# Order of a first tile's steps, longer warm-up, shift sums taken singly, and a fold split moved in a Fourier mixer layer

## The chip, the cores and the metric

The kernel runs on one core of one Trainium2 chip. The metric is device time in microseconds (us) of one execution, as the median of several; lower is better. The engines are called TensorE (PE in the profile, its weight loads PEld), VectorE (DVE), ScalarE (ACT), GpSimd (POOL) and SyncE (SP), which issues nearly all transfers.

## What is computed

One adaLN-modulated Fourier mixer layer on two sequences, 128 context tokens and 512 latent tokens of width 1024, each with a condition vector of its own:

```python
def modulation(cond, w_mod, b_mod):
    m = jax.nn.silu(cond) @ w_mod + b_mod
    shift, scale, gate = jnp.split(m[:, None, :], 3, axis=-1)
...
h = rms_norm(x, norm_w) * (1 + scale) + shift
u, z = jnp.split(h @ w_in, 2, axis=-1)          # w_in: 1024 x 2048
y = fourier_mix(u) * jax.nn.silu(z)             # real 2-D DFT over positions and 256 channels, 4 groups
return x + gate * (y @ w_out)                   # w_out: 1024 x 1024
```

All arrays are float32. Where full precision is wanted the kernel splits an operand into a high and a low part and makes three products (high x high, high x low, low x high).

## The kernel before, in words

The order of the work on every engine is written out by hand: each engine runs its instructions in the order in which the Python code issues them, and the framework only adds the semaphores. A helper `at(n, i, ...)` puts calls into a table, and `run(n, i)` issues them at that place of the loops over TensorE's products.

**First stage, z half of `w_in`, pieces 0 to 7** (lines 817 to 858). The width is cut into 8 tiles of 128. For each tile k there arrive `wm[k]` (512 KB of the scale weights), `xt[:, k]` (320 KB of transposed tokens) and piece k of `w_in` (256 KB, kept in `zs` for k < 5). From these come: `modulate(k)`, 16 small matmuls that give the scale (L285); `modulate_rows`, a ScalarE copy (L291); `modulate_columns`, 2 matmuls on TensorE (L295) and a VectorE step that gives `a8` (L296); `plain`, the high part of the scaled tokens `hh` (L329 on ScalarE; for tile 0 the 512 latent columns on VectorE, L325); `high_piece` and `low_piece`, the split of the weights into `wh` (L208, ScalarE, for tile 0 VectorE) and `wl` (L215, VectorE); `plain_low`, the low part `hl` (L336, VectorE). Then 12 matmuls of 512 columns (`product`, L358) and 3 for the context tokens (`product_ctx`, L368) per tile. The steps of tile u = k+1 are issued among the products of tile k. `ahead` says whether `modulate(u)` stands before or behind the first products of tile k; it is false for k = 0 and k = 6. `warm_up(n, cols)` issues matmuls on a tile of zeros (L269) whose result nobody reads.

**Shift sums.** The shift of each tile is a weighted sum taken on VectorE: `weigh_shift(k, j)` multiplies a 512 KB tile of weights with one of the two condition rows and accumulates (L302), and `finish_shift(k)` follows with three small steps (L310, L342, L343). `weigh_tile(k)` is two such sums and the finish. Tiles 0, 1 and 2 are weighed in the iterations k = 4, 5 and 6, behind `plain_low`; tiles 3 to 7 later. `load_shift(4)`, `(5)` and `(6)` reuse the memory of tiles 0, 1 and 2, so SP holds these transfers, and all behind them in its queue, until that tile is weighed.

**Second stage, pieces 8 to 15** (lines 890 to 926): 5 PSUM banks and 3 more hold 8 halves; `product_halves` fills them (L395). Beside it run the shift sums of tiles 3 to 7, the rms of the tokens, and the folds: `fold_pairs(q)` (8 VectorE steps) and `fold_split(q)`, which for each of 5 tables makes a ScalarE copy to f16 (L543) and a VectorE difference (L544), q being a quarter of the channels. `fold_piece(n)` is two VectorE steps on a piece of `w_in` (L201, L202), after which SP loads another piece. `take_halves(f, i)` copies a finished half from PSUM to `zs` (L442; VectorE for f = 1, ScalarE otherwise). `turn_shifts` makes 8 small matmuls (L421) into columns 256 to 263 of the bank that holds half (2, 1), and VectorE copies them out (L422). `sequence(k)` is 18 f16 matmuls (L569) into two PSUM tiles `pc` and `pl`, and `evacuate(k)` two ScalarE steps that empty them (L603). `sequence(0)` and `(1)` need fold quarter 0, `sequence(2)` quarter 1; `sequence(1)` takes over the PSUM tiles that `evacuate(0)` empties.

**The rest** (lines 929 to 1063): products for u (L609) with `sequence` between them, the channel transform, and the products with `w_out`, all of it TensorE work one behind the other.

Of the kernel before, what the change touches and what calls it, by code (L numbers as in the profile page):

```python
# [25 lines left out]
KT = D // P  # L26
# [78 lines left out]
def fourier_step(ctx: ExitStack, tc: tile.TileContext, a):  # L105
# [46 lines left out]
    def load_shift(k):  # L152
        if 0 <= k < KT:
            if k % 4 < 2:
                wr[k] = sp.tile([P, D], F32, name=f"wr{k}", tag="wr", bufs=2)
            else:
                wr[k] = folded[:, D * (k % 2) : D * (k % 2) + D]
            nc.sync.dma_start(wr[k], a["w_rows"][0, k])
# [9 lines left out]
    def load_piece(n):  # L168
        if n < 48 and n not in raw:
            c, k = place(n)  # L170
            src = a["w_in"][c, k] if c < 4 else a["w_out"][c - 4, k]
            if c == 0:
                if n < 5:
                    raw[n] = zs[:, 4:KT, :].rearrange("p e t -> p (e t)")[:, 512 * n : 512 * n + 512]
                else:
                    raw[n] = sp.tile([P, 512], F32, name=f"ws{n}", tag="wz", bufs=3)
                wz[n] = raw[n]
            else:
                raw[n] = wpool.tile([P, 512], F32, name=f"ws{n}", tag="ws")
            nc.sync.dma_start(raw[n], src)  # L180
# [24 lines left out]
    def high_piece(n, copy=nc.scalar.copy):  # L205
        if n < 48:
            hi = wpool.tile([P, 512], F32R, name=f"wh{n}", tag="wh")
            copy(hi, raw[n])  # L208
            wsplit[n] = (hi, None)

    def low_piece(n, engine=nc.vector):
        if n < 48:
            t, hi = raw.pop(n), wsplit[n][0]
            lo = wpool.tile([P, 512], F32R, name=f"wl{n}", tag="wl")
            engine.tensor_tensor(lo, t, hi, op=ALU.subtract)  # L215
            wsplit[n] = (hi, lo)
            if not (n < KT or 2 * KT <= n < 4 * KT):
                load_piece(n + 5)
# [48 lines left out]
    def warm_up(n, cols=512):  # L267
        for _ in range(n):
            nc.tensor.matmul(spare[:, 0:cols], idle[:, 0:P], idle[:, 0:cols], start=True, stop=True)  # L269
# [11 lines left out]
    def modulate(k):  # L281
        pm = pms[k % 2]
        for ko in range(KT):
            j = ko % 4
            nc.tensor.matmul(  # L285
                pm[32 * j : 32 * j + 32, 0:P], cs[:, ko, :], wm[k][:, ko, :], start=ko < 4, stop=ko >= 4
            )

    def modulate_rows(k):
        rows[k] = tmp.tile([P, P], F32, name="part")  # L290
        nc.scalar.copy(rows[k], pms[k % 2][:, 0:P])  # L291

    def modulate_columns(k):
        m = pms[k % 2][:, 256:258]
        nc.tensor.matmul(m, rows.pop(k), sel, start=True, stop=True)  # L295
        nc.vector.tensor_scalar(  # L296
            a8[:, k, :], m, b_scale[:, k : k + 1], nw8[:, k : k + 1], ALU.add, ALU.mult
        )

    def weigh(w, j, out):  # L300

        nc.vector.scalar_tensor_tensor(  # L302
            junk, w, 1.0, cb[:, D * j : D * j + D], ALU.mult, ALU.mult, accum_out=out
        )

    def weigh_shift(k, j):
        weigh(wr[k], j, sh[:, k, j : j + 1])

    def finish_shift(k):
        nc.vector.tensor_scalar(sh[:, k, :], sh[:, k, :], b_shift[:, k : k + 1], None, ALU.add)  # L310
        shift_columns(k, hs[k], T)
# [7 lines left out]
    def plain(k):  # L319
        hs[k] = tuple(  # L320
            xpool.tile([P, X_COLS], F32R, name=f"h{q}{k}", tag=f"a{q}") for q in "hl"
        )
        for j, cols in ((1, slice(0, SL)), (0, slice(SL, T))):
            if k == 0 and j:
                nc.vector.tensor_scalar(  # L325
                    hs[k][0][:, cols], xt[:, k, cols], a8[:, k, j : j + 1], None, ALU.mult
                )
            else:
                nc.scalar.activation(  # L329
                    hs[k][0][:, cols], xt[:, k, cols], AF.Identity, scale=a8[:, k, j : j + 1]  # L330
                )
# [8 lines left out]
    def shift_columns(k, parts, at):  # L340
        hi, lo = (x[:, at : at + 2] for x in parts)
        nc.vector.tensor_copy(hi, sh[:, k, :])  # L342
        nc.vector.tensor_tensor(lo, sh[:, k, :], hi, op=ALU.subtract)  # L343
# [9 lines left out]
    def product(n, f, act, passes=(0, 2, 1)):  # L353

        first, last = ends(n)
        for i in passes:
            w_, x_ = three(n, act)[i]
            nc.tensor.matmul(  # L358
                chunk(n // KT)[f], w_[:, P * f : P * f + P], x_[:, 0:SL],
                start=first and i == 0, stop=last and i == 1,  # L360
            )
# [427 lines left out]
    def go_ahead(k):  # L789
        if k < KT:  # L790
            load_scale(k)
            load_piece(k)
            load_tokens(k)
        if k == 3:
            load_cond()
        if k == KT:
            load_piece(KT)
            load_piece(KT + 1)
            load_shift(4)
            load_natural(0)  # L800
            nc.sync.dma_start(ident, a["ident"])
            load_natural(1)
        elif k > KT:
            load_shift(5)
            load_natural(2)
            for n in range(KT + 2, KT + 5):
                load_piece(n)
            load_natural(3)
        else:
            load_shift(k - 4)  # L810

    def weigh_tile(k):
        for j in range(2):
            weigh_shift(k, j)
        finish_shift(k)
# [3 lines left out]
    modulate(0)  # L819
    modulate_rows(0)  # L820
    warm_up(5, 128)
    high_piece(0, nc.vector.tensor_copy)
    modulate_columns(0)
    warm_up(6, 256)
    plain(0)
    low_piece(0)
    plain_low(0)
    for k in range(KT - 1):
        u = k + 1
        act = hs[k]  # L830
        ahead = 0 < k < KT - 2
        if ahead:
            modulate(u)
            modulate_rows(u)
        go_ahead(u + 2)
        for f in range(4):
            product(k, f, act, (0,))
        product_ctx(k, act, (0,))
        if not ahead:
            modulate(u)  # L840
            modulate_rows(u)
        high_piece(u)
        for f in range(2):
            product(k, f, act, (2,))
        modulate_columns(u)
        plain(u)
        low_piece(u)
        plain_low(u)
        if k == 2:
            silu_cond()  # L850
        if 3 < k:
            weigh_tile(k - 4)
        for f in range(2, 4):
            product(k, f, act, (2,))
        product_ctx(k, act, (2,))
        for f in range(4):
            product(k, f, act, (1,))
        product_ctx(k, act, (1,))
    k = KT - 1
    act = hs[k]  # L860
    high_piece(KT)
    low_piece(KT)
    load_shift(6)
    load_natural(4)
    product_ctx(k, act, (0,))
# [24 lines left out]
    for n, i, fn, *ms in (  # L890
        (8, 0, high_piece, 9), (8, 0, low_piece, 9), (8, 0, square, 0, 1), (8, 0, weigh_tile, 3), (8, 0, load_shift, 7),
        (8, 2, high_piece, 10), (8, 3, low_piece, 10), (8, 3, square, 2), (8, 3, load_tables),
        (9, 0, weigh_tile, 4), (9, 1, high_piece, 11), (9, 1, low_piece, 11), (9, 1, open_folds),
        (9, 1, weigh_tile, 5),
        (9, 2, square, 3), (9, 3, high_piece, 12, 13), (9, 3, low_piece, 12, 13), (9, 3, square, 4), (9, 3, rms),
        (10, 0, high_piece, 14), (10, 0, spread_rms), (10, 0, low_piece, 14), (10, 1, fold_first, 0),
        (11, 0, high_piece, 15), (11, 0, low_piece, 15), (11, 0, weigh_tile, 6, 7), (11, 0, fold_context, 0),
        (11, 2, fold_pairs, 0),
        (12, 1, fold_split, (0, "co", "so", "c", "ce", "se")),
        (12, 3, fold_first, 1), (12, 3, fold_context, 1),   # L900
        (14, 0, open_x, 0, 1, 2, 3), (14, 1, shift_products, 0, 1), (14, 1, order_rms), 
        (14, 1, take_halves, (0, 1), (0, 0), (3, 1)), (14, 1, fold_pairs, 1), (14, 1, fold_piece, 16), 
        (14, 2, take_halves, (3, 0)),  (14, 2, fold_piece, 17),
        (14, 2, fold_split, (1, "c", "co", "so", "se", "ce")),
        (14, 3, turn_shifts), (14, 3, load_gate, 0, 1), (14, 3, sequence, 0), (14, 3, take_halves, (1, 1), (2, 1), (1, 0)), (14, 3, evacuate, 0), (14, 3, fold_piece, 18),
    ):
        for m in ms or [()]:
            at(n, i, fn, *(m if type(m) is tuple else [m]))
# [33 lines left out]
    for n in range(16, 24):  # L942
        k = n - 16
# [187 lines left out]
```

## Time and profile before

| | us |
|---|---|
| median of 3 runs (lowest to highest) | 190.67 (190.64 to 191.15) |
| the profiled execution's own time | 192.47 |
| its span in the profile | 190.7 |

| engine | busy us | share of the span |
|---|---|---|
| PE | 182.9 | 96% |
| DVE | 145.3 | 76% |
| ACT | 87.8 | 46% |
| POOL | 16.8 | 9% |

The profile is of one execution. All times inside it count from the start of its span. "Busy" of PE is the union of its matmuls, whose starts are recorded and whose ends are modelled, so that one overlaps the next a little. "PEclk" is the share of TensorE's full clock, 2.4 GHz, that was granted in a stretch; the other level is 1.2 GHz. A number in brackets behind an instruction is the time for which its engine sat idle before it, and what ended that.

### The profile page before, as it was taken

The numbers are of one execution on the slowest core, as the hardware profiler recorded it, in microseconds if no ns is written. First come the engines' busy times: TensorE is split into PE (matmuls) and PEld (weight loads), VectorE is DVE, ScalarE is ACT, GpSimd is POOL, SyncE is SP. The second block draws the span as 40 slices with busy tenths as digits, with TensorE's granted clock in tenths as the row PEclk, the third lists the DMA queues.
The fourth block names the chain that finished last, engine by engine and source line by source line (L and its number), as shares of the span: only waits on it lengthen the run. The fifth ranks groups of instructions, "written<-read, shape, count | busy, mean of one in ns | idle before, by whom it ended". The sixth has DMA issues, their size and how long they took to land.

```text
span 190.7 us, 3251 instructions
## 1 busy us (share of the span) xinstructions
PE 182.9 (96%) x1162; PEld 147.5 (77%) x1162; DVE 145.3 (76%) x319; ACT 87.8 (46%) x195; POOL 16.8 (9%) x56
## 2 busy tenths in 40 slices
PE   7699999989999999799999999999999999999993
PEld 2467777768999979777767577677868889999993
DVE  0434435998999999969997696499869969999522
ACT  3133554347953039477626525868955127210000
POOL 3000000010033003700001103111110000000000
PEclk9879999999999999999999999999999999999999
DMA  5999999689983005752167613130142253712622
GB/s 187 354 410 405 404 401 403 232 295 366 348 283 141 8 3 155 236 229 64 52 199 216 235 58 107 55 110 5 58 108 57 83 181 137 241 76 109 238 106 100
DMA packets 15504, 35.55 MB, mean 186 GB/s; under 512 B 2432, under 2 KB 3200, under 8 KB 15360
## 3 DMA queue, kind: packets, MB, share of 16 engines
q1 hardware_dynamic: 15344, 35.30, 52.6%
q8 instruction: 9, 0.15, 0.4%
q10 hardware_dynamic: 144, 0.04, 0.1%
q14 instruction: 7, 0.06, 0.1%
HBM read 32.71 MB, written 2.62 MB: 185 GB/s over the span
## 4 chain that ended last, share of the span: by engine, by line
PE 65%; DVE 23%; ACT 5%; DMA 3%; issue 2%; SPq 1%; DVEq 0%
PE acc L358 21%; PE acc L609 14%; DVE junk L302 9%; PE h L395 8%; PE s L395 7%; PE acc L368 5%; PE pl L569 4%; DMA zs<-in_w_in 3%; DVE wl L215 2%; PE pm L285 2%; ACT hh L329 1%; DVE shz L310 1%; DVE hl L336 1%; PE acc L617 1%; PE pc L569 1%
## 5 line engine op out<-in xcount | busy, mean ns | idle before, releaser
L609 PE MATMUL acc<-x,folded 128*128 128x324 f32 (+1 forms) x128 | 37.0, 438 | 0.0
L609 PEld LDWEIGHTS acc<-x,folded 128*128 128x128 f32 x128 | 23.5, 190 | 9.6 <-issue 1.0
L215 DVE TENSOR_TENSOR wl<-ws,wh 128x512 fp32r<-128x512 f32 x27 | 17.9, 686 | 2.4 <-ACT wh L208 2.4
L302 DVE SCALAR_TENSOR_TENSOR junk<-wg,cb 128x1024 bf16<-128x1024 f32 x16 | 19.5, 1221 | 0.3
L208 ACT CAST wh<-ws 128x512 fp32r<-128x512 f32 x27 | 16.2, 616 | 7.6 <-PE h L395 7.5
L358 PE MATMUL acc<-yh,wh 128*128 128x512 f32 x32 | 13.1, 408 | 0.1
L358 PE MATMUL acc<-yl,wh 128*128 128x512 f32 x32 | 12.6, 394 | 0.0
L358 PE MATMUL acc<-yh,wl 128*128 128x512 f32 x32 | 12.6, 394 | 0.0
L329 ACT ACTIVATE hh<-xt,a 128x128 fp32r<-128x128 f32 (+1 forms) x15 | 7.5, 545 | 10.9 <-DVE a L296 10.9
L358 PE MATMUL acc<-hh,wh 128*128 128x512 f32 x32 | 10.3, 446 | 1.6 <-DVE hh L325 1.6
L296 DVE TENSOR_SCALAR a<-pm,b_scale,nw 128x2 f32<-128x2 f32 x8 | 2.2, 277 | 12.4 <-PE pm L295 12.4
L358 PE MATMUL acc<-hh,wl 128*128 128x512 f32 x32 | 11.1, 423 | 0.0
L395 PE MATMUL h<-hh,wl 128*128 128x256 f32 (+1 forms) x40 | 11.0, 292 | 0.0
L395 PE MATMUL h<-hl,wh 128*128 128x256 f32 (+1 forms) x40 | 11.0, 292 | 0.0
L395 PE MATMUL h<-hh,wh 128*128 128x256 f32 (+1 forms) x40 | 11.0, 292 | 0.0
L395 PE MATMUL h<-yh,wh 128*128 128x256 f32 (+1 forms) x40 | 11.0, 292 | 0.0
L395 PE MATMUL h<-yl,wh 128*128 128x256 f32 (+1 forms) x40 | 11.0, 292 | 0.0
L395 PE MATMUL h<-yh,wl 128*128 128x256 f32 (+1 forms) x40 | 11.0, 290 | 0.0
L302 DVE SCALAR_TENSOR_TENSOR junk<-folded,cb 128x1024 bf16<-128x1024 f32 x8 | 9.8, 1222 | 0.1
L302 DVE SCALAR_TENSOR_TENSOR junk<-wr,cb 128x1024 bf16<-128x1024 f32 x8 | 9.8, 1222 | 0.1
L358 PE MATMUL acc<-hl,wh 128*128 128x512 f32 x32 | 9.2, 393 | 0.0
L336 DVE SCALAR_TENSOR_TENSOR hl<-xt,a,hh 128x512 fp32r<-128x512 f32 (+1 forms) x16 | 8.1, 548 | 1.4 <-ACT hh L329 1.4
(212 smaller groups left out, 462.3 us busy)
## 6 DMA issues: line engine op xcount, KB each, us to landing
ws<-in_w_in SPq DMA_DIRECT2D x27, 256.0 KB, 4.5
wg<-in_w_rows SPq DMA_DIRECT2D x8, 512.0 KB, 3.4
ws<-in_w_out SPq DMA_DIRECT2D x16, 256.0 KB, 2.7
wm<-in_w_scale SPq DMA_DIRECT2D x7, 512.0 KB, 7.9
xt<-in_x_t SPq DMA_DIRECT2D x8, 320.0 KB, 7.7
xn<-in_x_nat SPq DMA_DIRECT2D x5, 512.0 KB, 6.1
out<-o SPq DMA_DIRECT2D x7, 320.0 KB, 2.2
wr<-in_w_rows SPq DMA_DIRECT2D x4, 512.0 KB, 6.9
```

The costliest lines, as they stand in the source:

```text
L208: copy(hi, raw[n])
L215: engine.tensor_tensor(lo, t, hi, op=ALU.subtract)
L285: nc.tensor.matmul(pm[32 * j : 32 * j + 32, 0:P], cs[:, ko, :], wm[k][:, ko, :], start=ko < 4, stop=ko >= 4)
L296: nc.vector.tensor_scalar(a8[:, k, :], m, b_scale[:, k : k + 1], nw8[:, k : k + 1], ALU.add, ALU.mult)
L302: nc.vector.scalar_tensor_tensor(junk, w, 1.0, cb[:, D * j : D * j + D], ALU.mult, ALU.mult, accum_out=out)
L329: nc.scalar.activation(hs[k][0][:, cols], xt[:, k, cols], AF.Identity, scale=a8[:, k, j : j + 1])
L336: nc.vector.scalar_tensor_tensor(hl[:, cols], xt[:, k, cols], a8[:, k, j : j + 1], hh[:, cols], ALU.mult, ALU.subtract)
L358: nc.tensor.matmul(chunk(n // KT)[f], w_[:, P * f : P * f + P], x_[:, 0:SL], start=first and i == 0, stop=last and i == 1,)
L368: nc.tensor.matmul(chunk(n // KT)[4], x_[:, SL:T], w_, start=first and i == 0, stop=last and i == 1)
L395: nc.tensor.matmul(half(c, f, j), w_[:, P * f : P * f + P], x_[:, tokens(c)[j]], start=first and i == 0, stop=last and i == 2,)
L569: nc.tensor.matmul(to, fold[source][x][rows, kk], t[rows, c : c + w], start=n == 0, stop=n == len(jobs) - 1)
L609: nc.tensor.matmul(chunk(n // KT)[f][:, 0 : cols.stop - cols.start], raw[n][:, P * f : P * f + P], xs[n % KT][:, cols], start=first, stop= ...
```

## The change

Five edits, all of order and place; the only added work is 8 matmuls on zeros.

1. Tile 0 on VectorE: `modulate_columns(0)` and `plain(0)` now stand ahead of `high_piece(0)`.
2. The last warm-up is 14 matmuls of 256 columns instead of 6.
3. The shift sums of tiles 0 to 2 become parts (tile i // 2, condition i % 2): part 0 in iteration 3, parts 1 and 2 in iteration 4, part 3 in 5, part 4 in 6, and part 5 behind `low_piece(8)` in the last tile's products.
4. `ahead` is true for k = 6 too: the scale of tile 7 stands before the products of tile 6.
5. In the second stage `take_halves(2, 1)` and `(1, 1)` go from behind `turn_shifts` and `sequence(0)` to the place (14, 2), before the last products of f = 1; `fold_split(1)` goes from (14, 2) to the end of (14, 3), behind `evacuate(0)` and `fold_piece(18)`; `take_halves(1, 0)` goes behind `evacuate(0)`.

```diff
+    def weigh_part(i):
+        weigh_shift(i // 2, i % 2)
+        if i % 2:
+            finish_shift(i // 2)
...
     warm_up(5, 128)
+    modulate_columns(0)
+    warm_up(14, 256)
+    plain(0)
     high_piece(0, nc.vector.tensor_copy)
-    modulate_columns(0)
-    warm_up(6, 256)
-    plain(0)
     low_piece(0)
     plain_low(0)
     for k in range(KT - 1):
         u = k + 1
         act = hs[k]
-        ahead = 0 < k < KT - 2
+        ahead = 0 < k
...
-        if 3 < k:
-            weigh_tile(k - 4)
+        for i in {3: (0,), 4: (1, 2), 5: (3,), 6: (4,)}.get(k, ()):
+            weigh_part(i)
...
     high_piece(KT)
     low_piece(KT)
+    weigh_part(5)
     load_shift(6)
...
-        (14, 2, take_halves, (3, 0)),  (14, 2, fold_piece, 17),
-        (14, 2, fold_split, (1, "c", "co", "so", "se", "ce")),
-        (14, 3, turn_shifts), (14, 3, load_gate, 0, 1), (14, 3, sequence, 0), (14, 3, take_halves, (1, 1), (2, 1), (1, 0)), (14, 3, evacuate, 0), (14, 3, fold_piece, 18),
+        (14, 2, take_halves, (3, 0), (2, 1), (1, 1)),  (14, 2, fold_piece, 17),
+        (14, 3, turn_shifts), (14, 3, load_gate, 0, 1), (14, 3, sequence, 0), (14, 3, evacuate, 0), (14, 3, take_halves, (1, 0)),
+        (14, 3, fold_piece, 18), (14, 3, fold_split, (1, "c", "co", "so", "se", "ce")),
```

## Rows read from the trace of the kernel before

**Rows 1.** Stretches of the span: start:end, length, busy us (instructions) per engine, clock, DMA.
```profile
4.80:8.20 3.40, 1.91 (x29) 1.21 (x21) 1.01 (x3) 0.67 (x2) 0.00 (x0) 1.00 0.97 335
8.20:11.60 3.40, 3.26 (x21) 2.09 (x21) 1.61 (x4) 0.00 (x1) 0.00 (x0) 0.50 1.04 408
...
46.00:79.00 33.00, 32.64 (x252) 31.02 (x251) 31.72 (x76) 17.34 (x42) 7.62 (x18) 1.00 0.54 175
...
80.00:187.60 107.60, 107.49 (x623) 86.55 (x620) 87.10 (x185) 50.15 (x112) 6.12 (x21) 1.00 0.37 125
```

**Rows 2.** Timeline of the first tile: start, duration, engine, line, instruction, [idle before].
```profile
1.19 3.17 PE L269 MATMUL spare<-idle 128*128 128x512 f16 x7 [1.19 <-DVE idle L232]
...
5.90 0.81 PE L269 MATMUL spare<-idle 128*128 128x256 f16 x6
...
7.15 0.43 DVE L208 CAST wh<-zs 128x512 fp32r<-128x512 f32 x1 [6.02 <-DMA zs<-in_w_in]
7.49 0.27 DVE L296 TENSOR_SCALAR a<-pm,b_scale,nw 128x2 f32<-128x2 f32 x1
...
7.80 0.49 DVE L325 TENSOR_SCALAR hh<-xt,a 128x512 fp32r<-128x512 f32 x1
...
8.34 2.08 PE L358 MATMUL acc<-hh,wh 128*128 128x512 f32 x4 [1.63 <-DVE hh L325]
...
11.74 0.73 PE L358 MATMUL acc<-hh,wl 128*128 128x512 f32 x2
```

**Rows 3.** Transfers of early tiles: issues on SP, and us from issue to landing.
```profile
1.65 0.42 SPq L162 DMA_DIRECT2D xt<-in_x_t  x1
2.59 0.43 SPq L150 DMA_DIRECT2D wm<-in_w_scale  x1
11.88 0.33 SPq L150 DMA_DIRECT2D wm<-in_w_scale  x1
...
xt<-in_x_t SPq DMA_DIRECT2D x1, 320.0 KB, 4.3
...
wm<-in_w_scale SPq DMA_DIRECT2D x1, 512.0 KB, 5.8
...
wm<-in_w_scale SPq DMA_DIRECT2D x7, 512.0 KB, 7.9
```

**Rows 4.** Timeline of TensorE in the next tile, same columns as rows 2.
```profile
14.44 0.64 PE L285 MATMUL pm<-wm,cs 128*32 128x128 f32 x16
...
16.28 0.63 PE L358 MATMUL acc<-hh,wl 128*128 128x512 f32 x2
```

**Rows 5.** Timeline from tile 5's scale to the start of tile 7.
```profile
30.52 0.28 DVE L296 TENSOR_SCALAR a<-pm,b_scale,nw 128x2 f32<-128x2 f32 x1 [2.38 <-PE pm L295]
...
38.86 1.22 DVE L302 SCALAR_TENSOR_TENSOR junk<-wr,cb 128x1024 bf16<-128x1024 f32 x1
...
40.68 0.27 DVE L296 TENSOR_SCALAR a<-pm,b_scale,nw 128x2 f32<-128x2 f32 x1
...
41.09 0.40 PE L368 MATMUL acc<-wh,hl 128*128 128x512 f32 x1
...
42.05 0.50 PE L368 MATMUL acc<-wh,hh 128*128 128x512 f32 x1 [0.57 <-ACT hh L329]
```

**Rows 6.** Timeline around `turn_shifts` and `sequence(1)`, by engine.
```profile
74.33 0.95 PE L421 MATMUL h<-small,shifts 128*128 128x2 f32 x8
...
78.29 0.34 PE L395 MATMUL s<-hh,wl 128*128 128x386 f32 x1
79.65 0.22 PE L569 MATMUL pl<-seq_h,co_h 128*128 128x128 f16 x1 [1.01 <-ACT x L603]
...
74.61 0.44 ACT L543 CAST c_h<-xn 128x256 f16<-128x256 f32 x1
...
78.95 0.37 ACT L442 COPY zs<-h 128x256 f32<-128x256 f32 x1 [2.48 <-DVE zs L422]
...
78.76 0.15 DVE L422 COPY zs<-h 128x8 f32<-128x8 f32 x1
```

## The prediction

> **What bounds the kernel now.** I read the table of stretches first. From 80 us to the end of the products TensorE is busy for 107.49 of 107.60 us, and from 46 to 79 us for 32.64 of 33.00 [rows 1]. So nothing late can be won without removing matmuls, which the change does not do; what can be won lies where TensorE stands still or runs slowly. Then I read the timelines of TensorE for gaps, and there are three. (1) The first tile: the warm-up ends at 6.7 us, the first product starts at 8.34 after 1.63 us of idleness [rows 2], and the granted clock, full from 4.8 to 8.2, is 0.50 (1.2 GHz) from 8.2 to 11.6 [rows 1]. In the 3.4 us before that fall TensorE was busy for 1.91 us. (2) At 42.05 us TensorE waits for tile 7's `hh` [rows 5]. (3) At 79.65 us `sequence(1)` waits for `evacuate(0)` [rows 6]. After 80 us a shift of everything in front passes unchanged to the end.
>
> **Edit 1, order on VectorE.** Today VectorE waits for piece 0, which has landed just before 7.15, then does the copy `wh` (0.43), the scale (0.27) and `hh` (0.49), and the product follows at 8.34 [rows 2]. The scale needs only TensorE's column step, which comes ahead of the 5.90 warm-up, so VectorE could do it at about 6.1. `hh` also needs the tokens, issued at 1.65 and landed 4.3 later, at 5.95 [rows 3]. In the new order scale and `hh` are through at about 6.9, under the wait for piece 0, and the copy runs from 7.15 to 7.58. The first product starts at about 7.62: **0.72 us earlier**.
>
> **Edit 2, warm-up.** 256 columns at 2.4 GHz take 0.107 us, so 14 matmuls from 5.90 end at about 7.4, inside the wait; their cost is nothing as long as they run at full clock, and the cover is the 0.2 us that is left to 7.62. The stretch from 4.8 to 8.2 will then be busy for about 2.9 of 3.4 us instead of 1.91. The clock had risen after a stretch filled like that (7 warm-ups over 3.17 us from 1.19 [rows 2]), so I take it that it does not fall at 8.2. What the fall costs is read at either level: from the first `hh,wh` to the third pass, five products of 512 columns and the 16 scale matmuls take 11.74 - 8.34 = 3.40 us [rows 2]; the same work of the next tile at full clock takes 16.28 - 14.44 = 1.84 [rows 4]. **1.56 us**, if no transfer is late: `wm[1]`, issued at 2.59, lands 5.8 later at 8.4 [rows 3], and is wanted at about 8.9. The next tiles' transfers are issued early: the one at 11.88, with 7.9 to land, is there by 19.8 [rows 3], and is wanted at some 21.0. Between 0 (the clock falls all the same) and 1.56 I take 1.56, since the stretch is closer to the filled one.
>
> **Edits 3 and 4, shift sums and `ahead`.** Today two sums and a finish stand between tile 6's work and tile 7's scale on VectorE. The second sum runs at 38.86 for 1.22 us, the scale comes at 40.68, and TensorE, whose last product started at 41.09, starts the next at 42.05 [rows 5]. A product of 512 columns is 0.21 us at full clock, so up to 0.96 - 0.21 = 0.75 us are lost (0.57 by the idle time alone, which takes modelled ends). VectorE's work is the same in sum. One sum moves into iteration 3, where VectorE idles for about 2.4 us per tile (2.38 before the scale at 30.52 [rows 5]), and one behind `low_piece(8)`. Iteration 4 has two sums and a finish and overruns a tile's 4.5 us by about half a microsecond, so tile 6's scale stays late by that much; but `modulate(7)` now stands before tile 6's products and fills 0.6 us in TensorE, so that nothing waits. Iteration 6 has one sum, begun after tile 7's `hl`. I take **0.75 us**, with 0.57 as the low end. On SP, `load_shift(4)`, `(5)` and `(6)` and what is queued behind them wait for tiles 0, 1 and 2. These are finished some 3 us earlier too, so no transfer of the second stage gets later against its use.
>
> **Edit 5, the fold split.** VectorE's 5 differences of `fold_split(1)` stand before `turn_shifts`' copy, which runs at 78.76. ScalarE's `take_halves(2, 1)` waits 2.48 us for that copy, `evacuate(0)` stands behind it on ScalarE, and TensorE, whose last product started at 78.29, starts `sequence(1)` at 79.65 [rows 6]. A product of 386 columns is 0.16 us, so 1.20 us are lost (1.01 by the idle time). With the split behind `evacuate(0)` this chain is gone: **1.20 us**. What is late next: quarter 1 of the fold is wanted only by `sequence(2)`, a round of TensorE's work later; I estimate that the differences end about 2 us ahead of it. But the edit adds a wait. `take_halves(2, 1)` reads the bank that `turn_shifts`' matmuls write, and now stands before them. ScalarE reaches that place at 74.61, when it begins the casts today, and the copy takes 0.37 [rows 6]; TensorE is ready at 74.33. It would start at about 75.03: **0.70 us back**, and all products stand queued behind. Between 0 (no order between the two) and 0.70 I take 0.70. For it speaks that today ScalarE's copy waits for VectorE's copy of other columns of that same bank, though both only read. The Trainium skill's page "PSUM — Partial Sum Buffer", section "PSUM bank collisions raise a hardware error", says that any two engines at one bank must be kept apart, reads against reads included. By that rule the 0.70 is due, and the trace's wait agrees with it; if only equal columns were kept apart, the sum would be 186.4.
>
> **Sum.** 0.72 + 1.56 + 0.75 + 1.20 - 0.70 = 3.53 us. The profiled execution took 192.47 us, its span of 190.7 and 1.8 around it; the median of the runs is 190.67. The profiled one would become 188.9, and the median 190.67 - 3.53 = **187.1 us**.
>
> **Rivals.**
> - *The clock gives nothing*, because it falls in spite of the longer warm-up, or did not fall in the unrecorded runs (they are 1.8 us shorter than the recorded one, which may be the recording alone). 187.1 + 1.56 = 188.7. For it: only one execution is seen. Against it: the stretch is filled as before the rise. Chance 0.16.
> - *The warm-up runs at 1.2 GHz*, because the clock rises later than at 4.8 in other executions. 14 times 0.213 from 5.90 ends at 8.9, 1.27 us behind 7.62: 188.4. The skill's page "TensorE: Matmul & The Clock Gate", part 1, says that the place of the rise differs from run to run; by that, some runs would be so. The three runs lie within 0.5 us. Chance 0.06.
> - *No wait at `turn_shifts`*: 187.1 - 0.7 = 186.4, if ScalarE's copy and TensorE's matmuls, in different columns, need no order. Chance 0.10.
> - *The head start is absorbed.* VectorE is busy for 31.72 of 33.00 us from 46 to 79 [rows 1]; if its chain kept its old times, TensorE would wait for it at `turn_shifts` and only edit 5 would be left: 190.67 + 0.70 - 1.20 = 190.2. Against it: VectorE starts that stretch behind TensorE's and ScalarE's last steps of the first stage, which come earlier by the same 3 us. Chance 0.06.
> - *Slower: the new wait at `turn_shifts` grows.* It lengthens one for one with any lateness of ScalarE behind VectorE's folds. The run is slower once the copy, which would end at 75.0 on the old clock, ends later than 74.33 + 1.20 + 0.57 = 76.1, that is when the fold chain is 1.1 us later than today in spite of the earlier start. 2 us later, it gives 190.67 + 2.0 + 0.70 - 1.20 = 192.2. It would take a shift sum, or a transfer held behind it on SP, that becomes late; the moved sums all come earlier, so I see none. Chance 0.04.
>
> **How the numbers follow.** The forecast has 0.58, with its own range of 186.8 to 187.7 from the ends 0.57 and 1.01. The range of 186.3 to 188.9 takes in the missing wait below and the two clock rivals above, and leaves out about 0.1. About 0.3% (0.6 us) is what a measurement of this kernel can tell from no change. The forecast, the two clock rivals and the missing wait are faster (0.90), the absorbed start is the same (0.06), the last is slower (0.04).
>
> **What the changed profile would show.** First product at 7.6 us, and a granted clock of 1.00 from 8.2 to 11.6 (a start at 7.6 with 0.50 behind it: the first rival; a start near 8.9: the second). Tile 7's first product near 39.0 with no idle time before it. The first stage ending some 3.0 us earlier. TensorE idle for about 0.7 us before L421, released by ScalarE's L442, at about 72.0; several microseconds there would be the absorbed start or the slower rival. `sequence(1)` at about 76.1 without a wait, and from there a constant shift to a span of about 187.2. I am wrong if a new wait stands between 46 and 80 us, or if the shift changes after 80.

## The result: 189.27 us, and the profile after

The changed kernel took 189.27 us in the median (188.94 to 189.36) beside 190.83 for the kernel before (190.64 to 191.15): ratio 0.9913, 95% interval 0.9894 to 0.9933, so 1.66 us less by the ratio (1.3 to 2.0). Forecast were 187.1 us and a range of 186.3 to 188.9. The direction was right, the size was under half of the 3.53 us that were forecast, and the time lies outside the range.

The odd thing is that the profile after is nearly the one that was forecast. Its span is 187.4 us (forecast about 187.2), its execution took 189.23. The span of before was 190.7, so the two profiles differ by 3.3 us, the two medians by 1.6. Each profiled execution is 1.8 us longer than its span; so the median of before, 190.83, belongs to a span of about 189.0, not of 190.7. Executions of the kernel before fall in two groups, one near 191 us and one from 192.35 up, and the profiled one was of the upper group.

The first tile after; the columns are start, duration, engine, line, instruction, [idle before]:

```profile
4.43 1.08 PE L285 MATMUL pm<-wm,cs 128*32 128x128 f32 x16
5.45 0.69 PE L269 MATMUL spare<-idle 128*128 128x128 f16 x5
...
6.17 1.69 PE L269 MATMUL spare<-idle 128*128 128x256 f16 x14
...
6.44 0.28 DVE L296 TENSOR_SCALAR a<-pm,b_scale,nw 128x2 f32<-128x2 f32 x1 [5.31 <-PE pm L295]
...
6.75 0.49 DVE L325 TENSOR_SCALAR hh<-xt,a 128x512 fp32r<-128x512 f32 x1
...
7.15 0.42 DVE L208 CAST wh<-zs 128x512 fp32r<-128x512 f32 x1
7.62 1.19 PE L358 MATMUL acc<-hh,wh 128*128 128x512 f32 x4
```

Beside [rows 2]: the first product starts at 7.62 as forecast, 0.47 us behind the start of the copy instead of 1.19, and four products take 1.19 us, not 2.08. The copy itself has no idle time before it any more: it follows `hh`, not the transfer, since the scale came at 6.44, 0.3 us later than I had worked out. In this execution the 16 scale matmuls took 1.08 us and ran at 1.2 GHz throughout; in the recorded one of before they took 0.76. The slack that I had left before the copy took this up, so that 7.62 came out all the same.

The stretches after (same columns as [rows 1]):

```profile
4.80:8.20 3.40, 3.40 (x40) 2.75 (x32) 1.69 (x4) 0.67 (x2) 0.00 (x0) 1.00 1.02 346
8.20:11.60 3.40, 3.40 (x30) 2.42 (x29) 1.98 (x6) 1.63 (x4) 0.00 (x0) 1.00 1.04 406
...
80.00:184.00 104.00, 103.89 (x595) 84.04 (x593) 85.32 (x180) 47.16 (x105) 6.11 (x21) 1.00 0.36 118
```

The granted clock stays at 1.00 where it was 0.50. From 80 us on TensorE is as full as before. Tile 7's start, then the place of `turn_shifts` and `sequence(1)`:

```profile
38.84 0.39 PE L368 MATMUL acc<-wh,hl 128*128 128x512 f32 x1
39.07 0.39 PE L368 MATMUL acc<-wh,hh 128*128 128x512 f32 x1
...
71.05 0.33 PE L395 MATMUL h<-hh,wl 128*128 128x386 f32 x1
71.97 1.05 PE L421 MATMUL h<-small,shifts 128*128 128x2 f32 x8 [0.59 <-ACT zs L442]
...
76.03 0.34 PE L395 MATMUL s<-hh,wl 128*128 128x386 f32 x1
76.21 0.23 PE L569 MATMUL pl<-seq_h,co_h 128*128 128x128 f16 x1
```

Against [rows 5] and [rows 6]: no wait for tile 7's `hh` (39.07, forecast 39.0); no wait before `sequence(1)` (76.21, forecast 76.1); and the new wait before L421, released by ScalarE's copy L442, at 71.97 (forecast 72.0). The lead over before is 79.65 - 76.21 = 3.44 us at `sequence(1)`, still 3.42 for matmuls at 160 us, and 3.28 for those at 167 us. So the sign "if the shift changes after 80" came in a small way: 0.14 us are lost there without a wait in the trace, and what took them is open.

### The profile page after: what moved, and what is told of

It reads as the page before. It is cut to its first block, busy times and chain, and to the rows that moved or that the text cites. A ratio compares the mean times of both kernels' runs of the same rounds, so it can differ in the third digit from the quotient of the medians.

```text
span 187.4 us, 3268 instructions
## 1 busy us (share of the span) xinstructions
PE 182.4 (97%) x1170; PEld 148.1 (79%) x1170; DVE 145.1 (77%) x319; ACT 87.6 (47%) x195; POOL 17.1 (9%) x56
## 4 chain that ended last, share of the span: by engine, by line
PE 76%; DVE 15%; ACT 6%; issue 1%; DVEq 0%
PE acc L358 25%; PE acc L609 14%; PE h L395 8%; PE s L395 8%; DVE junk L302 6%; PE acc L368 6%; PE pl L569 4%; PE spare L269 3%; PE pm L285 3%; DVE wl L215 2%; ACT zs L442 1%; PE pc L569 1%; PE acc L617 1%; ACT wh L208 1%; DVE shz L310 1%
## 5 line engine op out<-in xcount | busy, mean ns | idle before, releaser
L358 PE MATMUL acc<-hh,wh 128*128 128x512 f32 x32 | 9.4, 417 | 0.0
```

Of the source, the lines that this page charges most:

```text
L358: nc.tensor.matmul(chunk(n // KT)[f], w_[:, P * f : P * f + P], x_[:, 0:SL], start=first and i == 0, stop=last and i == 1,)
```

## The experiments

Two theories stood after the result. **A**: the fall of the clock belongs to the profiled execution, and most executions behind the median do not have it; its 1.56 us were taken off a time that did not contain them. **B**: the fall is in every execution, and the other terms were too large. Each kernel was run beside the kernel before on the same chip. The record has the mean granted clock of every execution: a fall to half for 3.4 of some 190 us makes it 0.991, and executions of before have either 0.991 and less or 0.997 and more. The ratios below are formed with executions of both groups. So the distance between the medians of the usual executions is given too, which are those with a mean clock of 0.997 or more and a time below 192 us; where the two differ, that distance is what an edit is worth.

**The kernel before, again.** No edit.

> The kernel before, unchanged, to see the span and the granted clock of many executions. Theory A (the fall of the clock at 8.2 us belongs to the one execution that the sum was made from): most executions have a span near 188.9 us, a mean clock of 0.999 or more and a time near 190.8; one with a mean clock near 0.991 would have a span near 190.7 and a time near 192.5. Theory B (the fall is in every execution, and other terms of the sum were too large): mean clock 0.991 in nearly all.

Twelve executions: five from 190.71 to 191.52, seven from 192.50 to 193.94, nothing between. The median of this set is 192.57, in the upper group, while only 4 of the 23 executions beside it are there (median 191.14); so the share changes from set to set. Over all sets of this study, the copy included, 100 timed executions of the kernel before lie so: 74 from 190.5 to 191.5 (median 191.0) and 26 from 192.35 up (median 192.7). Of the 96 whose clock is on record 23 have 0.982 to 0.991, all of them in the upper group; three of that group (192.35, 192.37 and 193.62) have 0.998 or more. The one recorded here is of the upper group, 193.94 with a span of 192.2. Its first copy and first product, and its stretches:

```profile
8.51 0.43 DVE L208 CAST wh<-zs 128x512 fp32r<-128x512 f32 x1 [7.38 <-DMA zs<-in_w_in]
...
9.70 1.20 PE L358 MATMUL acc<-hh,wh 128*128 128x512 f32 x4 [3.21 <-DVE hh L325]
```
```profile
4.10:10.90 6.80, 3.48 (x35) 2.28 (x34) 2.36 (x6) 0.89 (x4) 0.53 (x3) 1.00 1.01 366
10.90:14.30 3.40, 3.40 (x24) 2.50 (x23) 0.99 (x4) 1.18 (x3) 0.00 (x0) 0.51 1.05 413
```

The clock falls here too, but at about 10.9 us; piece 0 had landed some 1.4 us later (8.51 against 7.15), so that TensorE had been idle for 3.2 us before the first product. Theory A holds in its main point: the fall is not in every execution. It was not seen to be rare, though; a quarter have it, and in this set more than half.

**Longer warm-up alone.**

```diff
-    warm_up(6, 256)
+    warm_up(14, 256)
```

> The kernel before with 14 instead of 6 warm-up matmuls of 256 columns, nothing else. Theory A: the median stays within 0.3 us of before's (190.8), since there is no fall to prevent in most executions. Theory B: 1.5 us less, about 189.3. Third possibility: the warm-up runs at the low clock in part and delays the first product: up to 0.6 us more.

191.15 beside 191.14, ratio 1.0 (0.9985 to 1.0016); the usual executions beside it have 191.10. Theory B is out. But the eleven executions lie between 190.84 and 191.42, with none in the upper group; if a quarter of them were to have the fall, that would be luck about once in twenty such sets. So the edit probably does what it was costed for, in the executions that have the fall, and the median is not one of them. Its recorded execution is also what a profile of before without the fall looks like: its span is 189.5.

**No last warm-up.** The kernel before without the last 6 matmuls on zeros, to bring the fall about.

```diff
-    warm_up(6, 256)
```

> The kernel before without the last 6 warm-up matmuls, so that TensorE idles for about 2.4 us before the first product. If the fall of the clock follows from that idle time, nearly every execution has it: times near 192.5, a granted clock of 0.5 over some 3.4 us of the first two tiles, and 1.5 us more than the kernel before has in its usual executions (191.1). If the fall comes and goes for other reasons, the median stays at 191.1 with a few executions near 192.5, as before.

192.54 beside 191.03, ratio 1.009 (1.0061 to 1.0118), and 1.6 us above the usual executions (190.93); all eleven executions are at 192.28 or above. In the recorded one TensorE idles for 1.80 us before the first product, not for 2.4. Its stretches:

```profile
5.70:9.10 3.40, 1.60 (x11) 1.30 (x10) 2.13 (x5) 0.59 (x2) 0.00 (x0) 1.00 1.03 381
9.10:12.50 3.40, 3.40 (x23) 2.18 (x23) 0.78 (x4) 0.78 (x2) 0.00 (x0) 0.50 1.03 411
```

By the mean clock (0.991 or less) the fall is in 8 of 11 executions without the last warm-up, in 23 of 96 with 6 matmuls and in 0 of 11 with 14. Its price, between the groups' medians of before, is 1.7 us; the 1.56 of the sum was about right. The other three executions here (193.37, 193.61 and 193.82) have a mean clock of 0.999, like the three of before: they are long without a fall in the record, and why is open. A first rise that comes late would not show in that number, since the clock column reads 1.00 from the start, also over the first seven warm-ups of before (columns as in [rows 1]):

```profile
1.20:4.40 3.20, 3.15 (x7) 0.85 (x7) 0.00 (x0) 1.75 (x4) 0.69 (x4) 1.00 0.72 236
```

These seven matmuls of 512 columns take 3.17 us [rows 2], 0.45 each, about twice the 0.23 from one such product to the next at full clock (38.84 and 39.07 in the first section); so they ran at 1.2 GHz.

**The changed kernel with 6 warm-ups.**

```diff
-    warm_up(14, 256)
+    warm_up(6, 256)
```

> The changed kernel with the old 6 warm-up matmuls. Theory A: the median is that of the changed kernel, 189.2, within 0.3 us; single executions may still have a fall, since the first product comes at 7.6 and the idle time before it is shorter. Theory B: 1.5 us more, 190.8.

189.15 beside 191.14 (ratio 0.9894, 0.9867 to 0.992), 1.95 us below the usual executions, and none of its five above 189.43. No gain of the long warm-up is seen in the changed kernel: the new order of the first tile has already cut the idle time before the first product, to 0.63 us in the recorded execution:

```profile
7.15 1.19 PE L358 MATMUL acc<-hh,wh 128*128 128x512 f32 x4 [0.63 <-DVE wh L208]
```

**The first tile's order alone.**

```diff
-    high_piece(0, nc.vector.tensor_copy)
     modulate_columns(0)
     warm_up(6, 256)
     plain(0)
+    high_piece(0, nc.vector.tensor_copy)
```

> The kernel before with only the first tile's order on VectorE changed (scale and hh ahead of the copy wh), 6 warm-up matmuls as before. First product 0.47 us behind the start of the copy instead of 1.19, so 0.5 to 0.72 us less, 190.2 to 190.5 where before's usual executions have 191.0. If the shorter idle time (under 1 us) is enough to keep the clock up, no executions near 192; if the longer warm-up is needed for that, a quarter or more of them lie 1.6 us above the rest, as with the kernel before.

190.49 beside 191.19, ratio 0.9968 (0.9944 to 0.9993): 0.6 us less, by the ratio and against the usual executions (191.10). Twelve executions, all with a mean clock of 1.00; two of them, at 191.59 and 191.64, stand 1 us above the rest. With the two other sets that have the new order and 6 warm-ups (the one above and the first under "Both"), 23 executions show no fall. If a quarter were to have it, the chance of that would be 0.002; so the new order alone removes it or makes it rare.

**Shift sums and tile 7's scale alone.** The parts of the shift sums and `ahead = 0 < k`, as in the change; the rest as before.

> The kernel before with the shift sums taken singly and the scale of tile 7 ahead of tile 6's products, nothing else. If the wait for tile 7's hh is a term of the time: no idle time there and 0.75 us less than before (0.57 at least), about 190.3 where before has 191.1. If VectorE's fold chain keeps its old times (head start absorbed): less than 0.2 us, and more idle time at 79.6 us.

190.16 beside 191.03, ratio 0.9932 (0.9903 to 0.9961). Of twelve executions two have the fall (193.00, clock 0.991) and one is far off at 360.12 with a clock of 1.00; the nine usual ones have a median of 189.91, 1.0 us below the usual executions of before (190.93), where the sum had 0.75. Start of tile 7 and of `sequence(1)`, here and in the recorded execution of before with the longer warm-up, in which this part is unchanged; the first product starts at 8.39 in both:

```profile
39.83 0.39 PE L368 MATMUL acc<-wh,hh 128*128 128x512 f32 x1
...
77.33 0.22 PE L569 MATMUL pl<-seq_h,co_h 128*128 128x128 f16 x1 [1.04 <-ACT x L603]
```
```profile
40.65 0.50 PE L368 MATMUL acc<-wh,hh 128*128 128x512 f32 x1 [0.58 <-ACT hh L329]
...
78.29 0.22 PE L569 MATMUL pl<-seq_h,co_h 128*128 128x128 f16 x1 [1.07 <-ACT x L603]
```

TensorE has no idle time at tile 7 any more; the lead is 0.82 us there and 0.96 at `sequence(1)`.

**The second stage's copies and fold split alone.** The last lines of the change's diff, the rest as before.

> The kernel before with the places of the copies and of the fold split changed, nothing else. By the sum: the wait of 1.2 us before sequence(1) is gone, a wait of 0.6 to 0.7 before L421 is new, 0.5 us less in all, about 190.6 where before has 191.1. If the split only moves the wait to a later sequence: no change.

190.71 beside 191.03, ratio 0.9972 (0.9945 to 0.9999). Of twelve executions one has the fall (191.97, clock 0.991) and one is far off at 298.3 (clock 0.565); the ten usual ones have a median of 190.68, 0.25 us below the usual executions of before. TensorE around L421 and `sequence(1)`:

```profile
72.67 0.33 PE L395 MATMUL h<-hh,wl 128*128 128x386 f32 x1
73.62 1.05 PE L421 MATMUL h<-small,shifts 128*128 128x2 f32 x8 [0.61 <-ACT zs L442]
...
77.87 0.23 PE L569 MATMUL pl<-seq_h,co_h 128*128 128x128 f16 x1
```

In the recorded execution of before with the longer warm-up, where this part is unchanged:

```profile
72.74 0.34 PE L395 MATMUL h<-hh,wl 128*128 128x386 f32 x1
72.92 0.95 PE L421 MATMUL h<-small,shifts 128*128 128x2 f32 x8
```

The last products before L421 start at 72.67 and 72.74, so this execution is 0.07 us ahead when it comes to the edit. Less that, L421 starts 73.62 - 72.92 + 0.07 = 0.77 us late, and `sequence(1)`, at 77.87 instead of 78.29, is 0.42 - 0.07 = 0.35 us early: 1.12 us are won at `sequence(1)` and 0.77 given back at L421, where the sum had 1.20 and 0.70.

**The changed kernel, again.** No edit.

> The changed kernel, unchanged, for many executions: if the longer warm-up keeps the clock up, none or few of them lie 1.5 us above the rest, the median is 189.2, and the distance to before's usual executions is 1.9 to 2.0 us, the sum without the clock's term (0.72 + 0.75 + 1.20 - 0.70 = 1.97). If 1.97 is too large as well, about 1.5.

189.56 beside 191.03 (ratio 0.9902, 0.9866 to 0.9937). Of ten executions seven lie from 189.15 to 189.83, two at 190.55 and one far off at 203.2 (clock 0.853). Without the last the median is 189.52, 1.4 us below the usual executions of before; the seven alone have 189.25, 1.7 below. What the two at 190.55 are is open, as no recorded execution is among them; their mean clock, 0.997 and 1.00, shows no fall.

**Without the new wait.** `take_halves(2, 1)` behind `evacuate(0)`.

```diff
-        (14, 2, take_halves, (3, 0), (2, 1), (1, 1)),  (14, 2, fold_piece, 17),
-        (14, 3, turn_shifts), (14, 3, load_gate, 0, 1), (14, 3, sequence, 0), (14, 3, evacuate, 0), (14, 3, take_halves, (1, 0)),
+        (14, 2, take_halves, (3, 0), (1, 1)),  (14, 2, fold_piece, 17),
+        (14, 3, turn_shifts), (14, 3, load_gate, 0, 1), (14, 3, sequence, 0), (14, 3, evacuate, 0), (14, 3, take_halves, (1, 0), (2, 1)),
```

> The changed kernel with take_halves(2, 1) behind evacuate(0), so that the shift matmuls have no copy in front of them. If the 0.59 us of idle time before L421 is a term of the time, the span falls by 0.6 to 0.75 us, to about 186.7, and the time to about 188.6. If another wait takes its place (sequence(1) on ScalarE's later copies), less than 0.2 us is won and the trace shows TensorE idle near 75.5 or 76.4 us.

188.43 beside 191.14 (ratio 0.9872, 0.9833 to 0.9912), 0.7 below the changed kernel with 6 warm-ups on the same chip (189.15); one of the six executions stands alone at 190.54 (clock 0.998). In the recorded one L421 follows the products without idle time, and so does `sequence(1)`:

```profile
71.55 0.95 PE L421 MATMUL h<-small,shifts 128*128 128x2 f32 x8
...
75.69 0.23 PE L569 MATMUL pl<-seq_h,co_h 128*128 128x128 f16 x1
```

> The changed kernel with take_halves(2, 1) behind evacuate(0), a second time, beside the same runs of before as the order alone: 2.5 to 2.7 us less than before's usual executions, 188.3 to 188.5, that is 0.6 to 0.9 below the changed kernel's 189.2. If the first set of six was lucky: 189.0 or more.

A second set: 188.64 beside 191.19 (ratio 0.9867, 0.9822 to 0.9912), the highest of six at 189.59. This recorded execution shows what the longer warm-up can cost:

```profile
6.39 2.08 PE L269 MATMUL spare<-idle 128*128 128x256 f16 x14
...
7.36 0.42 DVE L208 CAST wh<-zs 128x512 fp32r<-128x512 f32 x1
8.22 1.17 PE L358 MATMUL acc<-hh,wh 128*128 128x512 f32 x4
```

The 14 matmuls took 2.08 us instead of 1.69, about what four of them at 1.2 GHz would add, and the first product came 0.44 us behind the end of the copy. This is the second rival, in part; of the five recorded executions with the new order and 14 warm-ups one more has it, by 0.1 us.

**Both.** The same with 6 and with 14 warm-ups, on one chip.

> The changed kernel with take_halves(2, 1) behind evacuate(0) and the old 6 warm-up matmuls. If 14 warm-ups are a cost where the clock rises late (in one execution the first product came 0.4 us behind the copy's end), the median is 0 to 0.4 us below the version with 14, at 188.1 to 188.5, with no executions 1.5 us above the rest, as the idle time before the first product is under 1 us. If the clock needs the longer warm-up, some executions lie near 190.

> The same with 14 warm-ups, for comparison on the same chip: 188.4 to 188.7.

188.26 beside 191.01 with 6 (ratio 0.9849, 0.9822 to 0.9876; six executions from 188.08 to 188.38), 188.35 with 14 (0.9858, 0.9827 to 0.9890; 188.04 to 188.88). The two are alike in the median, so the cost of the longer warm-up is not shown in time. Either version beats both kernels of the case: its ratios to before are 0.985 to 0.987, the changed kernel's 0.990 and 0.991. Beside the 0.7 us of the first set, on the chip of the second the late copy (188.64) was 0.9 us below the changed kernel with the same 14 warm-ups (189.52, another set).

## Why the prediction was wrong, point by point

- **The step that failed** is the carrying over: "The profiled one would become 188.9, and the median 190.67 - 3.53". The first half came to 189.23. The second took the clock's 1.56 us from a median in which there is no fall. What the runs showed in its place: by the mean granted clock the fall is in 23 of 96 executions of before, the median that was to be changed belongs to the others, and the longer warm-up alone moves the median by nothing (191.15 beside 191.14). That is 1.56 us of the 1.97 by which 3.53 was too much.
- The number that should have told it stood in the prediction: the profiled execution was 1.8 us longer than the median of three runs that agree within 0.5. I called that difference possibly "the recording alone". A recorded execution of the changed kernel takes 189.23 with a median of 189.27, so recording costs nothing here, and 1.8 us was near the fall's price of 1.56. The first rival said this and gave 188.7; it should have had most of the chance instead of 0.16. Even its 188.7 was 0.6 us short.
- Edit 1: 0.72 forecast, 0.6 measured alone. What was missed is that this edit by itself also takes away the fall (none in 23 executions with the new order and 6 warm-ups).
- Edit 2: the price of a fall was about right (1.56 forecast, 1.7 between the groups), its frequency was not asked for.
- Edits 3 and 4: 0.75 forecast, 1.0 alone (0.82 at tile 7 in the trace); no wait took its place.
- Edit 5: 1.20 - 0.70 = 0.50 forecast; 1.12 - 0.77 = 0.35 in the trace, 0.25 in time. The new wait came at its place, with its releaser and about its size. The Trainium skill's page "PSUM — Partial Sum Buffer", section "PSUM bank collisions raise a hardware error", has two engines at one bank kept apart, also in different columns; the trace agrees with it.
- Two figures of the working do not follow from their rows. The copy would end at 74.61 + 0.37 = 74.98, which gives 0.65 us and not 0.70; no row shows the other 0.05, and the wait came out longer than either. And the ends 0.57 and 1.01 give a range of 187.1 to 187.5, not of 186.8 to 187.7.
- The parts alone sum to 0.6 + 1.0 + 0.25 = 1.85 us without the clock (1.97 forecast). The change as a whole gave 1.56, 1.4 and, with 6 warm-ups, 1.95 between medians. Whether the 0.4 or more between the first two and the last is the longer warm-up's late products is open: two of five traces show such, by 0.1 and 0.4 us, the recorded execution behind the 189.23 does not, and the direct comparison shows nothing.
- The rivals on the head start, absorbed or turned into a growing wait, did not come: VectorE's chain moved with TensorE's. The first step of its last fold before L421 (L523) starts at 69.07 instead of 72.16, 3.09 us earlier, and TensorE's last product there 3.11 us earlier.

## What to carry to other kernels

Before a sum is made against a median, its profile must be of the same kind of execution: compare the profiled execution's own time with the others, and if the difference has the size of a term of the sum, take that term out or ask how often it is there. A change that removes a loss which fewer than half of the executions have shows in their spread, not in their median. A copy that was moved ahead of matmuls into the same PSUM bank turned into TensorE's wait here, and behind the work that it does not serve it cost nothing.

## What the runs showed of the hardware

After almost the same idle time the granted clock fell in one execution and not in another: the recorded one of before idled for 1.63 us before the first product and the clock fell at 8.2, the one with edit 5 alone idled for 1.62 us and it did not fall. One thing that differed is when the clock had risen. The clock column does not show a first rise (it reads 1.00 from the start), so it is worked out from durations: the 16 scale matmuls take 0.64 us at full clock and 1.08 at 1.2 GHz. First before, then edit 5 alone:

```profile
4.51 0.76 PE L285 MATMUL pm<-wm,cs 128*32 128x128 f32 x16 [0.16 <-ACT cs L247]
```
```profile
4.59 0.65 PE L285 MATMUL pm<-wm,cs 128*32 128x128 f32 x16 [0.23 <-ACT cs L247]
...
8.29 1.19 PE L358 MATMUL acc<-hh,wh 128*128 128x512 f32 x4 [1.62 <-DVE hh L325]
```

By that the clock rose at about 4.8 us in the first, where a part of them still ran slowly, and by 4.6 in the second. That this decided about the fall is not shown. Over the recorded executions the rise lies between about 3.8 us (the seven first warm-ups take 2.97 us instead of 3.17) and 7.2 us (part of the 14 from 6.39 on still slow, as shown above), though TensorE's first matmul started at 1.19 in all of them. The Trainium skill's page "TensorE: Matmul & The Clock Gate", part 1, says that the place of the rise differs from run to run, which these traces bear out; the half microsecond either way that it names is too little for them.
